# A hybrid mixer and feed-forward layer on one core: the down projection as seven products of half the size, on its whole depth, with its loads issued three products ahead

## The chip, the cores and the metric

The kernel runs on one core of one Trainium2 chip. The metric is the device time of one execution in microseconds (us), as the median of several executions on the chip. All arrays are fp32; a number that goes into a matmul is first split into a rounded part (hi, fp32r) and the rest (lo, fp32r), and one product of two tiles is three matmuls: hi by hi, hi by lo, lo by hi.

## The reference

One layer over 2048 tokens with 16 meta tokens ahead of them: a token mixer (a state-space branch and an mLSTM branch, merged and projected) and then a channel mixer. The change is in the channel mixer, and there in its last product:

```
def channel_mixer(x, g_pre, g_post, w_gate, w_up, w_conv, b_conv, w_down):
    h = rmsnorm(x, g_pre)
    a = causal_dwconv(h @ w_gate, w_conv, b_conv)
    y = (jax.nn.gelu(a, approximate=True) * (h @ w_up)) @ w_down
    return x + rmsnorm(y, g_post)
```

h has 1024 columns, w_gate and w_up are 1024 by 2816, w_down is 2816 by 1024. Below, y stands for the 2816-wide product that goes into w_down.

## The kernel before

The program is written in Python with a scheduler behind it: the order of the instructions on each engine is not the written one, but what the scheduler makes of it ahead of time. On the chip each engine then runs its own queue strictly in that order, with semaphores between the queues. All DMAs are issued by SP (the SyncE queue), in its order; an issue that has to wait holds up every issue behind it.

The mixer takes the first half of the program and is not touched. The feed-forward part has three stages.

- **Two passes of gate and up** (the loops over `m` in `range(NF)`, lines 1279 to 1303). Pass `p` takes half of the tokens; unit `m` makes 128 of the 2816 columns of y for them. Gate and up together are done by Strassen's algorithm: seven products named 1, 6, 2, 7, 5, 4, 3 instead of eight (`ffn_unit`, lines 1196 to 1262). In pass 0 each product is 24 matmuls that move 258 or 256 columns (two pieces of 12), in pass 1 it is 12 matmuls that move 512 columns. The activations are resident in 14 tiles `t0` to `t11`, `q0`, `q1`; the weights of each unit are loaded (`wg`, `wu`, lines 1131 and 1133), combined on VectorE and split on ScalarE and VectorE (lines 1124 and 1125). Each unit ends with a convolution, a Gelu and a product, in two halves, each stored to `y_d` in DRAM (line 1262).
- **The down projection** (lines 1311 to 1359). For each half `nh` of the output columns all 22 weight tiles of 128 by 512 are loaded through `mk`, split, and kept in `t0` to `t10`. Then for each of 16 token tiles three loads of y (8, 8 and 6 tiles of 128 by 128; `ys`, line 1335, two buffers) are split (`yhl`, ScalarE on line 1338, VectorE on line 1339), and 66 matmuls (lines 172 to 174) that move 512 columns add into one PSUM tile.
- **The end of each token tile** (lines 1344 to 1359): a square with sum, the gain, and for the second half the norm, `h1_d` loaded as a tile of 128 by 1024 and added, and two stores.

The tiles `mk` (three buffers of 128 by 2080), `dw` (tags `ws`, `wh`, `wl`, two buffers each) and `du`, `dx` (the units' own) share the on-chip memory with the 14 resident tiles. The helper `mm3` emits the three matmuls of a product, `mm3x` the same for Strassen's sums.

## Time and profile before

| | us |
|---|---|
| median of 3 runs | 2793.52 (2791.82 to 2795.34) |
| the profiled execution, its own time | 2792.36 |
| its span, first to last instruction | 2790.6 |
| TensorE busy in the span | 2759.1 |
| VectorE / ScalarE busy | 1761.1 / 1054.7 |
| gate and up, pass 0: first matmul | 1403.8 |
| gate and up, pass 1: last convolution starts | 2304.7 |
| down projection: first matmul to start of the last | 2287.3 to 2783.3 |

In a row of a window table stand the window, its length, then for PE (matmuls), PEld (weight loads of TensorE), DVE (VectorE), ACT (ScalarE) and POOL (GpSimd) the busy time and in brackets the number of instructions, then the granted clock of TensorE as a share of full speed, the busy share of the DMA engines and GB/s. Matmuls overlap each other in the array, so the duration of one is no measure of the rate; the count in a window without idle time is. In an answer on one line or tile, three durations in ns stand as smallest, middle and largest.

### The profile page before, as it was taken

The page shows a single profiled execution, that of the slowest core. Times are in us where ns is not written, and L with a number is a line of the kernel's source. Part 1 is how long each engine was busy: PE and PEld are TensorE (multiplying, and loading weights), DVE is VectorE, ACT ScalarE, POOL GpSimd, SP SyncE. Part 2 cuts the span into 40 slices and gives each one's busy share as a digit, 9 for nine tenths or more (in the row PEclk, how much of TensorE's full clock was granted, in tenths as well). Part 3 has the DMA queues.
Part 4 walks back from the last instruction along what each step waited for, and adds up shares of the span by engine and source line. Part 5 has one row for each costly group of instructions (what it writes and reads, how often), then busy time and mean ns, then how long its engine had stood idle before and what let it go on. Part 6 is the DMA issues. An engine that isn't in the chain of part 4 may idle for free.

```text
span 2790.6 us, 40815 instructions
## 1 busy us (share of the span) xinstructions
PE 2759.1 (99%) x15590; PEld 2484.9 (89%) x15590; DVE 1761.1 (63%) x3429; ACT 1054.7 (38%) x1979; POOL 136.8 (5%) x225
## 2 busy tenths in 40 slices
...
GB/s 309 106 79 131 158 147 121 71 69 72 145 159 144 167 212 121 223 196 250 265 157 138 159 234 87 73 176 85 80 80 81 79 145 149 99 90 165 157 166 128
DMA packets 323478, 395.47 MB, mean 142 GB/s; under 512 B 40321, under 2 KB 229142, under 8 KB 322642
## 3 DMA queue, kind: packets, MB, share of 16 engines
...
## 4 chain that ended last, share of the span: by engine, by line
PE 82%; DMA 7%; DVE 6%; ACT 1%; issue 1%; POOL 1%; SPq 0%; DVEq 0%; POOLq 0%; ACTq 0%
PE mm L172 10%; PE mm L174 10%; PE mm L173 10%; PE ac L173 9%; PE ac L174 9%; PE ac L172 8%; PE ac L179 4%; PE ac L178 4%; PE ac L177 4%; PE mm L177 3%; PE mm L179 3%; PE mm L178 3%; DMA wu<-in_w_up_dram 2%; DMA gat<-gab_d 1%; DVE w L1125 1%
## 5 line engine op out<-in xcount | busy, mean ns | idle before, releaser
L174 PE MATMUL mm<-hTh,wl 128*128 128x410 f32 (+3 forms) x1216 | 428.0, 352 | 0.0
L172 PE MATMUL mm<-hTh,wh 128*128 128x410 f32 (+3 forms) x1216 | 427.6, 352 | 0.0
L173 PE MATMUL mm<-hTl,wh 128*128 128x410 f32 (+3 forms) x1216 | 427.4, 352 | 0.0
L1339 DVE TENSOR_TENSOR yhl<-ys,yhl 128x1024 fp32r<-128x1024 f32 (+1 forms) x96 | 109.1, 1137 | 291.9 <-ACT yhl L1338 291.9
L173 PE MATMUL ac<-t,yhl 128*128 128x512 f32 x704 | 278.5, 396 | 0.0
L174 PE MATMUL ac<-t,yhl 128*128 128x512 f32 x704 | 277.3, 394 | 0.0
L172 PE MATMUL ac<-t,yhl 128*128 128x512 f32 x704 | 276.6, 393 | 0.0
L177 PE MATMUL mm<-t,w 128*128 128x258 f32 (+2 forms) x792 | 253.7, 321 | 3.5 <-DVE u L1226 2.6
L178 PE MATMUL mm<-t,w 128*128 128x258 f32 (+2 forms) x792 | 253.5, 320 | 0.4 <-DVE t L1069 0.4
L177 PE MATMUL ac<-t,w 128*128 128x258 f32 (+2 forms) x792 | 253.2, 320 | 0.6 <-ACT u L1217 0.6
L179 PE MATMUL ac<-t,w 128*128 128x258 f32 (+2 forms) x792 | 253.1, 320 | 0.1
L179 PE MATMUL mm<-t,w 128*128 128x258 f32 (+2 forms) x792 | 252.5, 320 | 0.7 <-DVE w L1125 0.7
L178 PE MATMUL ac<-t,w 128*128 128x258 f32 (+2 forms) x792 | 253.1, 320 | 0.0
L173 PEld LDWEIGHTS mm<-hTl,wh 128*128 128x128 f32 x1216 | 228.7, 188 | 2.6
L174 PEld LDWEIGHTS mm<-hTh,wl 128*128 128x128 f32 x1216 | 228.8, 188 | 2.3
L172 PEld LDWEIGHTS mm<-hTh,wh 128*128 128x128 f32 x1216 | 228.7, 188 | 2.0
L1338 ACT ACTIVATE yhl<-ys 128x1024 fp32r<-128x1024 f32 (+1 forms) x96 | 95.0, 990 | 348.4 <-PE ac L173 345.9
L156 ACT ACTIVATE wh<-ws 128x1024 fp32r<-128x1024 f32 x104 | 109.9, 1059 | 237.8 <-PE mm L173 137.5
L1124 ACT ACTIVATE w<-s 128x512 fp32r<-128x512 f32 x176 | 109.3, 628 | 164.7 <-DVE s L1139 70.3
L177 PEld LDWEIGHTS mm<-t,w 128*128 128x128 f32 x792 | 149.7, 189 | 18.0 <-DVE u L1226 4.4
L172 PEld LDWEIGHTS ac<-t,yhl 128*128 128x128 f32 x704 | 132.4, 188 | 32.3
L177 PEld LDWEIGHTS ac<-t,w 128*128 128x128 f32 x792 | 149.2, 189 | 13.0 <-ACT u L1217 1.1
...
## 6 DMA issues: line engine op xcount, KB each, us to landing
ys<-y_d SPq DMA_DIRECT2D x64, 512.0 KB, 3.7
wg<-in_w_gate_dram SPq DMA_DIRECT2D x44, 512.0 KB, 3.6
wu<-in_w_up_dram SPq DMA_DIRECT2D x44, 512.0 KB, 4.3
...
ws<-in_w_m_dram SPq DMA_DIRECT2D x32, 512.0 KB, 3.8
ws<-in_w_ba_dram SPq DMA_DIRECT2D x32, 512.0 KB, 4.0
ws<-in_w_out_dram SPq DMA_DIRECT2D x32, 512.0 KB, 5.3
gat<-gab_d SPq DMA_DIRECT2D x48, 256.0 KB, 4.8
```

The costliest lines, as they stand in the source:

```text
L156: S.activation(wh, ws, AF.Copy, scale=scale)
L172: T.matmul(out=ps, lhsT=lh, rhs=rh, start=first, stop=False)
L173: T.matmul(out=ps, lhsT=lh, rhs=rl, start=False, stop=False)
L174: T.matmul(out=ps, lhsT=ll, rhs=rh, start=False, stop=last)
L177: T.matmul(out=ps, lhsT=lh, rhs=rh, start=first, stop=False, skip_group_check=True)
L178: T.matmul(out=ps, lhsT=lh, rhs=rl, start=False, stop=False, skip_group_check=True)
L179: T.matmul(out=ps, lhsT=ll, rhs=rh, start=False, stop=last, skip_group_check=True)
L1124: S.activation(t[:, 0], src, AF.Copy)
L1125: V.tensor_tensor(t[:, 1], src, t[:, 0].bitcast(F32), ALU.subtract)
L1338: S.activation(yh, ys, AF.Copy)
L1339: V.tensor_tensor(yl, ys, yh.bitcast(F32), ALU.subtract)
```

## The change

The down projection is done by Strassen's algorithm. The 2816 rows of w_down are cut in two halves of 11 tiles, and its columns within each half `nh` in two halves of 256; two token tiles that lie four apart are taken together. Seven products (in the order 1, 6, 2, 7, 5, 4, 3) then stand for eight. One product is 11 tiles deep: 33 matmuls that move 256 columns. There are 2 halves of 8 units of 7, so 112 products.

What the products need is made ahead:

- `down_weight_sums`: in pass 0 of gate and up, units 1 to 4 and 14 to 21, the four sums of weight blocks are made on VectorE and stored to `wt_d`.
- `down_input_sums`: in pass 1, the four sums of y blocks are made and stored to `s_d`, one depth tile in each unit. The last one (`last_sums`) is made inside the down projection, since its y comes last.
- `turn_down`: while the last unit of pass 1 runs, 8 of the 11 weight tiles of six products are loaded through `mk` and split into `t0` to `t11`. The other 3 tiles of each product (`rest_piece`, tiles `x1` to `x7`) and product 3's 8 (`main_piece`, `q0`, `q1`) come in the down projection's first products. For the second half of the columns all 21 pieces are loaded again inside the stage, over the products that end the first half and begin the second, as the list `cut` deals them out.

The pools `mk` and `dw` are now closed ahead of the down projection, and a new pool `dn` takes their place. In it lie three buffers `raw` of 128 by 1408 through which everything passes that is split: the input of each product (128 by 1408 from `y_d` or `s_d`), the weight pieces (128 by 1024 and 128 by 768), and the two tiles of `last_sums`; and two tiles `st0`, `st1` of split input, which products take in turn. `st_load(i + 3)` is issued at product `i`, `st_split(i + 1)` too. The output of the first half of the columns goes to `yo_d` in DRAM and is read back (`y0`, one buffer) by `finish`, which reads `h1_d` in two halves through one buffer `ht`; the stores wait in the list `later` until products 1 and 3 of what follows.

The core of the diff (the removed stage is shown above):

```diff
+    s_d = dp.tile([8, 4, 128, 11, 128], F32, name="s_d")
+    wt_d = dp.tile([2, 4, 128, 11, 256], F32, name="wt_d")
+    yo_d = dp.tile([16, 128, 512], F32, name="yo_d")
...
+    def down_input_sums(p, m):
+        t = mk_tile()[:, 0:2048]
+        for h in range(2):
+            P.dma_start(out=t[:, h * 1024:h * 1024 + 1024], in_=y_d[m + 11 * h, :, p * 1024:(p + 1) * 1024])
+        yield
+        a11, a21, a12, a22 = (t[:, i * 512:i * 512 + 512] for i in range(4))
+        V.tensor_tensor(a22, a21, a22, ALU.add)
+        V.tensor_tensor(a21, a11, a21, ALU.subtract)
+        V.tensor_tensor(a11, a22, a11, ALU.subtract)
+        V.tensor_tensor(a12, a12, a11, ALU.subtract)
+        yield
+        for i, a in enumerate((a11, a21, a12, a22)):
+            P.dma_start(out=s_d[p * 4:p * 4 + 4, i, :, m, :].rearrange("j p t -> p j t"),
+                        in_=a.rearrange("p (j t) -> p j t", j=4))
...
+    ORDER = (1, 6, 2, 7, 5, 4, 3)
...
+    def split(hi, lo, raw):
+        S.activation(hi, raw, AF.Copy)
+        V.tensor_tensor(lo, raw, hi.bitcast(F32), ALU.subtract)
...
+    def turn_down():
+        for n in ORDER[:6]:
+            t = mk_tile()[:, 0:2048]
+            P.dma_start(out=t.rearrange("p (k n) -> p k n", k=8), in_=down_src(0, n, 0, 8))
+            places(n)
+            for h in range(2):
+                main_split(n, h, t[:, h * 1024:h * 1024 + 1024])
...
-        ffn_unit(1, m, op1, wt)
+        i = m - 1 if m < 12 else m - 12
+        piece_turn(down_input_sums(int(m >= 12), i) if m else None)
+        ffn_unit(1, m, op1, wt, turn_down if m == NF - 1 else None)
+        piece_sums()
+    piece_turn(None)
     phX.close()
-    el = pool(ctx, "el", bufs=2)
+    phM.close()
+    phW.close()
...
+    dn = pool(ctx, "dn")
+
+    PR = [(nh, j, n) for nh in range(2) for j in range(8) for n in ORDER]
...
+    def raw_tile():
+        return dn.tile([128, 1408], F32, tag="raw", name="raw", bufs=3)
...
+    def st_split(i):
...
+        st = dn.tile([128, 2, 1408], F32R, tag=f"st{turn_[0] % 2}", name="st")
+        split(st[:, 0], st[:, 1], raw_of.pop(i))
...
+    def rest_piece(nh, n):
+        raw = raw_tile()[:, 0:768]
+        P.dma_start(out=raw.rearrange("p (k n) -> p k n", k=3), in_=down_src(nh, n, 8, 11))
+        wrest[n] = dn.tile([128, 2, 768], F32R, tag=f"x{n}", name=f"x{n}")
+        split(wrest[n][:, 0], wrest[n][:, 1], raw)
...
+        def prod(ps, n, first):
+            i = PR.index((nh, j, n))
+            st_load(i + 3)
+            for f in before(i):
+                f()
+            st_split(i + 1)
+            st = st_of.pop(i)
+            for k in range(11):
+                mm3x(ps, st[:, 0, k], st[:, 1, k], moving(n, 0, k), moving(n, 1, k), first and k == 0, k == 10)
+            if n in (1, 3):
+                while later:
+                    later.pop(0)()
...
+    def finish(t, o1):
+        sm = dn.tile([128, 1], F32, tag="sm", name="sm", bufs=2)
+        V.tensor_reduce(out=sm, in_=sq4[t], op=ALU.add, axis=mybir.AxisListType.X)
+        rs = rstd_of(Small(dn, "r", 2), sm, 128, 1, 1.0 / D)
+        y0 = dn.tile([128, 512], F32, tag="y0", name="y0")
+        P.dma_start(out=y0, in_=yo_d[t])
+        for hh, src in ((1, o1), (0, y0)):
+            cs_ = slice(hh * 512, hh * 512 + 512)
+            ht = dn.tile([128, 512], F32, tag="ht", name="ht")
+            P.dma_start(out=ht, in_=h1_d[NM + t * 128:NM + (t + 1) * 128, cs_])
+            V.scalar_tensor_tensor(src, src, rs, ht, ALU.mult, ALU.add)
+            later.append(lambda cs_=cs_, src=src: P.dma_start(out=out[t * 128:(t + 1) * 128, cs_], in_=src))
...
+        if i < 6:
+            q = ORDER[i + 1]
+            f = [lambda: rest_piece(0, q)]
+            if i in (3, 4):
+                f.append(lambda: main_piece(0, 3, i - 3))
+        elif i in (9, ):
+            f = [last_sums]
+        elif first_i < i < last_i + 7:
+
+            f = second[cut[i - first_i - 1]:cut[i - first_i]]
...
+    cut = [0, 0, 2, 3, 5, 6, 8, 9, 12, 14, 16, 18, 21, 21]
```

Three places show how the order of the instructions changes. The first is VectorE's queue where pass 1 of gate and up ends. Before, from the last sum that waits for a product of gate and up (line 1236) on; `yhl` is the split of y for the down projection, and the first two of these stand ahead of this row:

```order
L1329 TENSOR_TENSOR t10_22848<-mk_22846,t10_22848 128x512 x2
L1261 TENSOR_TENSOR cc_22745<-cc_22745,u1_22650 128x512
L1236 TENSOR_TENSOR gp_22646<-ac_22705,u2_22651 128x512
L1256 SCALAR_TENSOR_TENSOR cc_22752<-gp_22646,cwf_89,cc_22752 128x512 x2
L1339 TENSOR_TENSOR yhl_22945<-ys_22942,yhl_22944 128x1024
L1261 TENSOR_TENSOR cc_22752<-cc_22752,u3_22652 128x512
```

Now, from the same sum (line 1276, after product 3 of the last unit) to the split of the first product's input; `t9` and `t11` are weights that `turn_down` splits, `mk_23001` the sums of y:

```order
L1276 TENSOR_TENSOR gp_23004<-ac_23063,u2_23009 128x512
L1155 TENSOR_TENSOR mk_23001<-mk_23001 128x512
L1381 TENSOR_TENSOR t9_23138<-mk_23135,t8_23137 128x1024
L1156 TENSOR_TENSOR mk_23001<-mk_23001 128x512
L1381 TENSOR_TENSOR t9_23138<-mk_23135,t8_23137 128x1024
L1296 SCALAR_TENSOR_TENSOR cc_23158<-gp_23004,cwf_92,cc_23158 128x512
L1381 TENSOR_TENSOR t11_23146<-mk_23143,t10_23145 128x1024
L1296 SCALAR_TENSOR_TENSOR cc_23158<-gp_23004,cwf_92,cc_23158 128x512
L1381 TENSOR_TENSOR t11_23146<-mk_23143,t10_23145 128x1024
L1301 TENSOR_TENSOR cc_23158<-cc_23158,u3_23010 128x512
L1381 TENSOR_TENSOR st_23182<-raw_23180,st_23182 128x1408
L1381 TENSOR_TENSOR st_23209<-raw_23185,st_23209 128x1408
```

Four splits and two sums now stand between the last sum of gate and up and its last product (line 1301), and no split of input stands ahead of it. On SP the same end, before, with the first loads of y for the down projection (`ys`) between the last stores of y:

```order
L1335 DMA ys_22854<-y_d_71 128x8x128
L1322 DMA mk_22822<-in_w_down_dram 128x4x512
L1335 DMA ys_22884<-y_d_71 128x8x128
L1262 DMA y_d_71<-cc_22599 128x512
L1322 DMA mk_22834<-in_w_down_dram 128x4x512
```

and now:

```order
L1302 DMA y_d_71<-cc_23151 128x512
L1159 DMA s_d_72<-mk_23001 128x4x128 x3
L1302 DMA y_d_71<-cc_23158 128x512
L1426 DMA raw_23180<-y_d_71 128x11x128
L1428 DMA raw_23185<-s_d_72 128x1408
L1426 DMA raw_23187<-y_d_71 128x11x128
L104 DMA g4_23194<-in_g_ffn_post_dram 128x512
L1546 DMA ht_25954<-h1_d_66 128x512
L1449 DMA raw_23189<-in_w_down_dram 128x3x256
L1428 DMA raw_23202<-s_d_72 128x1408
L1449 DMA raw_23204<-wt_d_73 128x768
```

The first load of input now stands behind the very last store of y, `cc_23158`; the weight rests (line 1449) alternate with inputs from then on. The second place is SP where the weights of the second half of the columns come in. Before, four loads of 128x4x512 and one of 128x2x512 (three of them shown) between loads of y:

```order
L1335 DMA ys_24329<-y_d_71 128x8x128
L1322 DMA mk_24297<-in_w_down_dram 128x4x512
L1335 DMA ys_24359<-y_d_71 128x8x128
L1322 DMA mk_24309<-in_w_down_dram 128x4x512
L1322 DMA mk_24321<-in_w_down_dram 128x2x512
```

Now, the first twelve of a stretch of 32 loads into `raw` (11 inputs on lines 1426 and 1428, 21 weight pieces on lines 1442 and 1449):

```order
L1426 DMA raw_25383<-y_d_71 128x11x128
L1442 DMA raw_25385<-in_w_down_dram 128x4x256
L1442 DMA raw_25391<-in_w_down_dram 128x4x256
L1428 DMA raw_25434<-s_d_72 128x1408
L1449 DMA raw_25436<-in_w_down_dram 128x3x256
L1426 DMA raw_25479<-y_d_71 128x11x128
L1442 DMA raw_25481<-wt_d_73 128x1024
L1442 DMA raw_25487<-wt_d_73 128x1024
L1428 DMA raw_25531<-s_d_72 128x1408
L1535 DMA yo_d_74<-o_25297 128x512
L1449 DMA raw_25533<-wt_d_73 128x768
L1426 DMA raw_25578<-y_d_71 128x11x128
```

Each of these loads takes one of the same three buffers. The third place is the end of SP's queue, about the last inputs. Before:

```order
L1335 DMA ys_25874<-y_d_71 128x8x128
L1355 DMA ht_25938<-h1_d_66 128x1024
L1335 DMA ys_25904<-y_d_71 128x6x128
L1359 DMA out_0_dram<-ht_25837 128x512 x2
L1359 DMA out_0_dram<-ht_25938 128x512 x2
```

and now:

```order
L1428 DMA raw_28069<-s_d_72 128x1408
L1548 DMA out_0_dram<-y0_27936 128x512
L1546 DMA ht_28197<-h1_d_66 128x512
L1542 DMA y0_28195<-yo_d_74 128x512
L1546 DMA ht_28200<-h1_d_66 128x512
L1548 DMA out_0_dram<-o_27944 128x512
L1548 DMA out_0_dram<-y0_28195 128x512
L1546 DMA ht_28250<-h1_d_66 128x512
L1542 DMA y0_28248<-yo_d_74 128x512
L1546 DMA ht_28253<-h1_d_66 128x512
L1548 DMA out_0_dram<-o_27945 128x512
L1548 DMA out_0_dram<-y0_28248 128x512
```

Loads of `ht` and `y0`, each into the one buffer of its name, now stand between the stores.

210 lines of the change are left out of this document (156 added, 54 removed).

## The prediction

> **What bounds the kernel now.** I read the profile's page first, then windows of single stages, then the rows of the instructions that the change makes larger or moves.
>
> ```profile
> span 2790.6 us, 40815 instructions
> PE 2759.1 (99%) x15590; PEld 2484.9 (89%) x15590; DVE 1761.1 (63%) x3429; ACT 1054.7 (38%) x1979; POOL 136.8 (5%) x225
> PE 82%; DMA 7%; DVE 6%; ACT 1%; issue 1%; POOL 1%; SPq 0%; DVEq 0%; POOLq 0%; ACTq 0%
> ```
>
> TensorE is busy for 99% of the span and holds 82% of the chain that ends last. The windows tell at which rate it works: one in pass 0 of gate and up, one in pass 1, one in the down projection, and the last.
>
> ```profile
> core 0: us, PE busy (x) PEld busy (x) DVE busy (x) ACT busy (x) POOL busy (x), PEclk, DMA share, GB/s
> 1750.00:1800.00 50.00, 50.00 (x420) 50.00 (x419) 37.45 (x73) 20.42 (x36) 0.56 (x3) 1.00 0.27 85
> 2100.00:2150.00 50.00, 50.00 (x217) 40.36 (x216) 33.62 (x54) 18.76 (x31) 2.19 (x2) 1.00 0.26 82
> 2400.00:2450.00 50.00, 50.00 (x217) 40.44 (x216) 13.87 (x14) 12.28 (x18) 0.00 (x0) 1.00 0.32 95
> ```
>
> Without idle time a matmul that moves 512 columns takes 50/217 = 0.2304 us, one that moves 256 or 258 takes 50/420 = 0.1190. The down projection waits for nothing today: VectorE is busy for 13.9 of 50 us there, ScalarE for 12.3.
>
> **The gain.** The old stage is three groups of 704 matmuls, of which this is one:
>
> ```profile
> L173 PE MATMUL ac<-t,yhl 128*128 128x512 f32 x704 | 278.5, 396 | 0.0
> ```
>
> That is 2112 x 0.2304 = 486.6 us. The new one is 112 products of 33, 3696 x 0.1190 = 439.8 us. **Gain: 46.8 us**, if TensorE still waits for nothing. One product lasts 33 x 0.1190 = 3.93 us.
>
> **What a tile costs on its way in.** Each tile in `raw` is loaded, rounded on ScalarE and subtracted on VectorE; only then can its buffer be loaded anew. The durations for 768 (smallest) and 1024 columns (middle), and the landing times:
>
> ```profile
> L1338 ACT ACTIVATE yhl<-ys x96: 831/1060/1064, 2277.5 to 2773.8; 128x1024 fp32r<-128x1024 f32 x64, 128x768 fp32r<-128x768 f32 x32
> L1339 DVE TENSOR_TENSOR yhl<-ys,yhl x96: 949/1226/1227, 2285.9 to 2774.7; 128x1024 fp32r<-128x1024 f32 x64, 128x768 fp32r<-128x768 f32 x32
> ys<-y_d SPq DMA_DIRECT2D x64, 512.0 KB, 3.7
> ys<-y_d SPq DMA_DIRECT2D x32, 384.0 KB, 3.2
> out_dram<-ht SPq DMA_DIRECT2D x32, 256.0 KB, 2.2
> wi<-win_d SPq DMA_DIRECT2D x8, 256.0 KB, 2.5
> ```
>
> ScalarE adds 229 ns and VectorE 277 ns for 256 columns, so 1408 columns are estimated at 1.40 and 1.64 us; 128 KB more add 0.5 us, so the 704 KB of an input land in an estimated 4.4. The turnover of a buffer is then 4.4 + 1.40 + 1.64 = 7.4 us for an input, 3.7 + 1.06 + 1.23 = 6.0 for 128x1024 of weights, 3.2 + 0.83 + 0.95 = 5.0 for 128x768.
>
> In the steady state three buffers hold: 7.4 us is less than three products (11.8). A split begins when the product two back has ended, and needs 1.40 + 1.64 = 3.0 us, at most 0.4 more for a copy ahead of it, against 3.93: it hides too. So units 2 to 6 of the first half should run at TensorE's rate. The stalls are elsewhere, in seven terms.
>
> **1. The gap between the stages.** The rows of a sum, a convolution step and two plain operations of 512 columns on VectorE:
>
> ```profile
> L1256 DVE SCALAR_TENSOR_TENSOR cc<-gp,cwf,cc 128x512 f32<-128x512 f32 x88 | 66.0, 749 | 8.7 <-ACT cc L1254 8.5
> L1261 DVE TENSOR_TENSOR cc<-cc,u 128x512 f32<-128x512 f32 x44 | 30.3, 688 | 0.1
> L1138 DVE TENSOR_TENSOR s<-wu 128x512 f32<-128x512 f32 x44 | 30.5, 693 | 52.2 <-DMA wu<-in_w_up_dram 52.2
> ```
>
> By the order, after the last matmul of gate and up VectorE does four operations of 0.69 (sum, two of `mk`, the last product), two of 0.75 and four weight splits of 1.23: 2.8 + 1.5 + 4.9 = 9.2 us. The last of these frees the store of `cc_23158`, and only behind that store does SP issue the first input: 4.4 + 1.40 + 1.64 = 7.4 more, all with TensorE idle. 16.6 us and issues, say 17; bounds 15 (part of the weight splits ready ahead) and 22 (the weight loads late, as they wait in the same queue). Today the inputs are loaded ahead of the last stores and this costs nothing. The idle clock adds to it:
>
> ```profile
> 1370.00:1375.00 5.00, 2.05 (x10) 1.39 (x9) 5.00 (x8) 1.06 (x1) 2.33 (x1) 1.00 0.99 348
> 1375.00:1380.00 5.00, 5.00 (x16) 3.93 (x17) 4.21 (x7) 0.65 (x2) 2.85 (x3) 0.66 0.48 148
> ```
>
> After 3 us of idle time the granted clock is 0.66 over the next 5 us, with 16 matmuls where 22 fit: 1.4 to 1.7 us lost. I take **18 us** for the gap.
>
> The Trainium skill (TensorE: Matmul & The Clock Gate, Part 1: The HAM clock gate) has the same rule: about 3.4 us of idle time halve the clock until some 3.4 us of work have passed. It would charge about 1.7 us for each such gap, and the two rows agree.
>
> **2. The first weights.** In the first seven products 7 inputs, 7 rests and 2 pieces of product 3 pass through three buffers: (7 x 7.4 + 7 x 5.0 + 2 x 6.0)/3 = 33 us against 7 x 3.93 = 27.5. That is 5.5 if no buffer ever waits. One does: an input that has landed holds its buffer until the product two back frees its `st`. With two buffers left, input and rest one after another take 12.4/2 = 6.2 us a product, 16 us over seven. I take **12**.
>
> **3. The last sums** (product 3 of the second unit). A y tile loads (3.7), four sums (4 x 0.69 = 2.8), a store (2.2), the input loads again from `s_d` (4.4), and splits (3.0): 16 us in a row. It begins when the input of product 7 has been split, so 7 and 4 lie beside it: 7.9. **9 us** with what VectorE's sums delay; bounds 4 and 14.
>
> **4. The second weights.** 14 pieces of 1024, 7 of 768 and 11 inputs pass through the three buffers: (14 x 6.0 + 7 x 5.0 + 11 x 7.4)/3 = 67 us, dealt out over products 51 to 61, which last 11 x 3.93 = 43. So 24 us if nothing waits; weights also wait for the last product that reads their place, and one queue holds up the next. **28 us**; bounds 15 (an early start) and 40.
>
> **5. The second half's norm.** `finish` adds to SP's queue two `y0`, four `ht` and four stores a unit, which wait for VectorE and for each other; an input behind them has about 3 us of slack. By the order the split of line 1547 that waits for `ht` also stands ahead of sums that TensorE waits for. No row shows this; from 0 to 3.5 us a unit over seven units (one 256 KB landing of 2.5 and one operation of 0.75), nearer the middle: **12 us**, bounds 0 and 25. No gain is possible, since nothing is taken out there.
>
> **6. The tail.** Today, from the last matmul:
>
> ```profile
> 2783.34 0.39 PE L174 MATMUL ac<-t,yhl 128*128 128x512 f32 x1
> 2785.57 0.55 POOL L107 TENSOR_TENSOR rs<-ms,neghalf 128x1 f32<-128x1 f32 x1 [13.50 <-DVE ms L105]
> 2786.16 1.41 DVE L1358 SCALAR_TENSOR_TENSOR ht<-o,rs,ht 128x512 f32<-128x512 f32 x2 [0.73 <-POOL rs L107]
> 2786.94 0.99 SPq L1359 DMA_DIRECT2D out_dram<-ht  x2
> ```
>
> 6.9 us to the span's end. Now two tiles end at once, with one `ht` and one `y0`: three loads in a row (2.5 and 0.4 of issue each) and two operations of 0.75 more: **10 us**; bounds 8 and 13.
>
> **7. Gate and up.** Four more sums of 0.69 in 12 units of pass 0 (20 us each) and in 21 of pass 1 (19.4 us each): VectorE's 37.5 of 50 us in pass 0 become 37.5 + 4 x 0.69 x 50/20 = 44.4, its 33.6 in pass 1 40.7. Under 90%, so mostly hidden; but its queue runs later. **4 us**, bounds 0 and 12.
>
> Sum: -46.8 + 18 + 12 + 9 + 28 + 12 + 10 + 4 = **+46 us**. The profiled execution took 2792.36 (1.8 around its span), 1.2 below the median of 2793.52; so 2838.6 for a profile, and 2839.7 as a median: **2840 us**. All low ends together (15, 5.5, 4, 15, 0, 8, 0 = 47.5) give no change; all high ends (22, 16, 14, 40, 25, 13, 12 = 142) give 2889.
>
> **The rivals.**
>
> *The loads keep ahead.* If landings are short, the buffers turn over in time: in the second weights, 32 tiles in 43 us leave 4.0 us a tile and buffer, where 6.3 are needed, so a load would have to land 2.3 us sooner than the rows say. For it: DMA is busy for a third of the time today, so there is room. Against it: the waits are of one load after another, not of volume. With terms 2 to 5 and 7 gone, 2793.5 - 46.8 + 28 = 2775 us. Chance 0.14.
>
> *The clock falls in every stall.* Slower still: if the 3 us gaps of terms 2, 3 and 4, about a dozen, each cost the 1.7 us of the rows above on the path, 20 us come on top: 2860. Against it: where loads set the pace, slower matmuls hide in part. Chance 0.10. The Trainium skill's rule quoted above (TensorE: Matmul & The Clock Gate, Part 1: The HAM clock gate) speaks for this one.
>
> *The change does not do what it says.* The loads are issued three products ahead only if a buffer is free; if SP's queue itself is the bound in the second half, inputs come late in every product there, 2 us each over 49 products: 2840 + 98 - 12 = 2926. The slack of 3 us speaks against it. Chance 0.04. Terms that happen to cancel within 0.2% (5.6 us, about what a measurement of this kernel can tell from no change): 0.04.
>
> **How the numbers follow.** The forecast has 0.68 and holds 2800 to 2885. Faster is the first rival, 0.14; the same 0.04; slower the rest, 0.68 + 0.10 + 0.04 = 0.82. The range leaves out the first and the third rival: 2795 to 2885.
>
> **What would show it.** Right: in the profile after, TensorE at 3696 matmuls of 0.119 us; a gap of some 17 us ahead of the first of them; idle time before matmuls on the tiles `x` and `t` in the first and the eighth unit, released by VectorE's split, and none in units 2 to 6; a clock below 1 behind the gap; 17 us from the last matmul to the end. Wrong: a stage of under 460 us from its first matmul to its last, or stalls spread evenly over all units.

## The result, and the profile after

The changed kernel takes 2913.8 us (median of 4 runs, 2909.45 to 2916.42), the kernel before 2792.7 beside it: a ratio of 1.0431, 95% interval 1.0413 to 1.0449. It is slower by 121 us. The forecast was 2840 (2795 to 2885), slower with a chance of 0.82: the side is right, the size is not. Its profiled execution has a span of 2913.9 us, 123.3 more than before's 2790.6.

The page of the changed kernel, the lines that answer to those of before (span; busy time of the engines; the chain that ended last):

```profile
span 2913.9 us, 45019 instructions
PE 2763.7 (95%) x17174; PEld 2563.7 (88%) x17174; DVE 1966.3 (67%) x3691; ACT 1138.1 (39%) x2073; POOL 134.2 (5%) x225
PE 58%; DMA 20%; DVE 15%; ACT 3%; issue 3%; SPq 1%; POOL 0%; DVEq 0%; ACTq 0%; POOLq 0%
```

TensorE's share of the chain fell from 82% to 58%; transfers (20%) and VectorE (15%) took it. The windows tell where. Gate and up, two windows each in pass 0 and pass 1; then the down projection in a quiet stretch, at its start, where the second weights come in, and in the second half:

```profile
1450.00:1500.00 50.00, 45.43 (x364) 44.79 (x363) 41.56 (x81) 20.08 (x38) 3.70 (x5) 0.97 0.83 271
1750.00:1800.00 50.00, 50.00 (x420) 50.00 (x419) 37.27 (x72) 22.13 (x41) 0.56 (x3) 1.00 0.25 80
1900.00:1950.00 50.00, 46.29 (x188) 35.78 (x187) 41.45 (x69) 16.38 (x27) 3.68 (x2) 0.97 0.97 301
2100.00:2150.00 50.00, 50.00 (x217) 40.51 (x216) 34.05 (x55) 18.35 (x31) 2.19 (x2) 1.00 0.30 99
2450.00:2500.00 50.00, 50.00 (x426) 50.00 (x425) 27.82 (x30) 21.01 (x30) 0.00 (x0) 1.00 0.66 201
2350.00:2375.00 25.00, 20.36 (x123) 19.25 (x123) 10.11 (x9) 8.88 (x11) 0.00 (x0) 0.76 0.65 206
2625.00:2675.00 50.00, 34.15 (x169) 30.63 (x167) 24.06 (x27) 18.50 (x23) 0.55 (x1) 0.62 0.61 197
2700.00:2800.00 100.00, 91.99 (x722) 90.25 (x721) 54.17 (x73) 36.58 (x51) 3.23 (x6) 0.95 0.73 232
```

Read the matmul counts. 420, 217 and 426 are the full rates, so the quiet windows (1750, 2100, 2450) run as forecast, the last a little faster (the forecast had 420). The others do not: in 1900:1950 there are 188 matmuls, where before had, in the same window,

```profile
1900.00:1950.00 50.00, 50.00 (x216) 40.50 (x215) 33.59 (x55) 18.87 (x31) 2.19 (x2) 1.00 0.25 77
```

In that window the changed kernel has a DMA share of 0.97 where before had 0.25, and VectorE at 41.5 of 50 us where it had 33.6: the sums of eleven units run within five, from 1884 to 1970 us. The gap between the stages, on TensorE and on SP:

```profile
2334.05 0.40 PE L182 MATMUL ac<-q,w 128*128 128x512 f32 x1
2351.03 0.58 PE L180 MATMUL ac<-t,st 128*128 128x256 f32 x1 [16.59 <-ACT st L1380]
```

```profile
2343.58 0.33 SPq L1302 DMA_DIRECT2D y_d<-cc  x1
2344.01 0.38 SPq L1426 DMA_DIRECT2D raw<-y_d  x1
```

16.6 us idle, and the first load of input 0.4 us behind the last store of y, as forecast. VectorE's queue ahead of that store, from its last sum for gate and up to their last product, takes 9.1 us (forecast 9.2):

```profile
2334.48 0.69 DVE L1276 TENSOR_TENSOR gp<-ac,u 128x512 f32<-128x512 f32 x1 [0.30 <-PE ac L182]
2342.86 0.69 DVE L1301 TENSOR_TENSOR cc<-cc,u 128x512 f32<-128x512 f32 x1
```

The durations that the forecast estimated (input splits on VectorE and ScalarE, input loads):

```profile
L1381 DVE TENSOR_TENSOR st<-raw,st 128x1408 fp32r<-128x1408 f32 x112 | 181.7, 1624 | 110.0 <-ACT st L1380 109.7
L1380 ACT ACTIVATE st<-raw 128x1408 fp32r<-128x1408 f32 x112 | 154.1, 1378 | 200.1 <-PE mm L182 76.6
raw<-s_d SPq DMA_DIRECT2D x64, 704.0 KB, 4.6
raw<-y_d SPq DMA_DIRECT2D x48, 704.0 KB, 4.5
```

1.62, 1.38 and 4.5 us against estimates of 1.64, 1.40 and 4.4: the inputs were priced right. The other loads were not. From 2330 us on, as medians of the few landings that the trace has, weight pieces of 512 KB took 4.7 and 6.3 us (the forecast took 3.7 from other loads), those of 384 KB 3.4 and 3.8 (3.2), and `ht` 4.4 (2.5):

```profile
raw<-wt_d SPq DMA_DIRECT2D x8, 512.0 KB, 4.7
raw<-in_w_down_dram SPq DMA_DIRECT2D x8, 512.0 KB, 6.3
raw<-wt_d SPq DMA_DIRECT2D x8, 384.0 KB, 3.4
raw<-in_w_down_dram SPq DMA_DIRECT2D x6, 384.0 KB, 3.8
ht<-h_d SPq DMA_DIRECT2D x32, 256.0 KB, 4.4
```

More was wrong in how the parts meet. A stall in a unit of the second half shows it, VectorE and then TensorE:

```profile
2775.30 0.75 DVE L1547 SCALAR_TENSOR_TENSOR o<-o,rs,ht 128x512 f32<-128x512 f32 x1 [0.60 <-POOL rs L110]
2776.66 1.63 DVE L1381 TENSOR_TENSOR st<-raw,st 128x1408 fp32r<-128x1408 f32 x1 [0.60 <-ACT st L1380]
2779.27 0.75 DVE L1547 SCALAR_TENSOR_TENSOR y<-y,rs,ht 128x512 f32<-128x512 f32 x1 [0.99 <-DMA ht<-h_d]
2780.02 0.42 DVE L1514 TENSOR_TENSOR o<-mm,o 128x256 f32<-128x256 f32 x1
```

```profile
2780.50 0.38 PE L180 MATMUL mm<-t,st 128*128 128x256 f32 x1 [2.03 <-DVE o L1514]
```

VectorE waits for `ht`; the sum of line 1514 stands behind it; TensorE waits 2.0 us for that sum. In the tail the same operations wait one after another for one buffer:

```profile
2897.42 0.75 DVE L1547 SCALAR_TENSOR_TENSOR o<-o,rs,ht 128x512 f32<-128x512 f32 x1 [0.60 <-POOL rs L110]
2901.52 0.75 DVE L1547 SCALAR_TENSOR_TENSOR y<-y,rs,ht 128x512 f32<-128x512 f32 x1 [3.35 <-DMA ht<-h_d]
2905.88 0.75 DVE L1547 SCALAR_TENSOR_TENSOR o<-o,rs,ht 128x512 f32<-128x512 f32 x1 [3.61 <-DMA ht<-h_d]
2909.89 0.75 DVE L1547 SCALAR_TENSOR_TENSOR y<-y,rs,ht 128x512 f32<-128x512 f32 x1 [3.26 <-DMA ht<-h_d]
```

**The account, term by term.** From the starts of the matmuls in the timeline I take, for each stretch, its length less the number of its matmuls times 0.1190 us; call that its *loss* (idle time and slow clock together). A unit has 231 matmuls. Before, the down projection alone would begin at 2297.0 (its last matmul's start, 2783.34, less 2111 x 0.2304); after, gate and up let go of TensorE at 2334.3 (2334.05 and one matmul).

| term | forecast, with bounds | measured | how |
|---|---|---|---|
| gain of the matmuls | -46.8 | -46.8 | at the forecast's two rates (see below); units 3 to 7 run without loss (-1.2 in all) |
| 7, gate and up | 4 (0 to 12) | 37 | 2334.3 - 2297.0 |
| 1, gap, with its slow clock | 18 (15 to 22) | 20 | 16.7 idle, 3.3 slow |
| 2, first weights | 12 (5.5 to 16) | 16.5 | loss of unit 1, 19.8, less the 3.3 |
| 3, last sums | 9 (4 to 14) | 11 | loss of unit 2 |
| 4, second weights | 28 (15 to 40) | 46 | loss of products 50 to 64 |
| 5, second half's norm | 12 (0 to 25) | 28 | loss of products 65 to 112 |
| 6, tail | 10 (8 to 13) | 12 | 19.5 from the last matmul's start to the end, 7.3 before |

These add up, with the -1.2, to 123: the difference of the spans. Three terms make the miss: gate and up (33 too little), second weights (18) and the norm (16).

The two rates in this table are the forecast's, counts of a window of 50 us, and such a count takes in the matmuls that reach over its edges. By the starts of the matmuls the spacing is 0.2323 us before (from 2303.10 to 2783.34) and 0.1180 after (units 3 to 7). By these the gain is 54 us and not 47, the down projection alone would have begun at 2292.9 before, so term 7 is 41, and each unit loses 0.2 more; the total is the same.

### The profile page after: what moved, and what is told of

Same layout as the page of the kernel before. It is cut to its first block, busy times and chain, and to the rows that moved or that the text cites. A ratio compares the mean times of both kernels' runs of the same rounds, so it can differ in the third digit from the quotient of the medians.

```text
span 2913.9 us, 45019 instructions
## 1 busy us (share of the span) xinstructions
PE 2763.7 (95%) x17174; PEld 2563.7 (88%) x17174; DVE 1966.3 (67%) x3691; ACT 1138.1 (39%) x2073; POOL 134.2 (5%) x225
## 4 chain that ended last, share of the span: by engine, by line
PE 58%; DMA 20%; DVE 15%; ACT 3%; issue 3%; SPq 1%; POOL 0%; DVEq 0%; ACTq 0%; POOLq 0%
PE mm L175 9%; PE mm L177 9%; PE mm L176 9%; PE ac L182 4%; PE ac L180 4%; PE ac L181 4%; PE mm L180 3%; PE mm L181 3%; PE mm L182 3%; DMA wu<-in_w_up_dram 3%; PE ac L176 2%; PE ac L177 2%; PE ac L175 2%; DVE w L1165 2%; DMA mk<-y_d 2%
## 5 line engine op out<-in xcount | busy, mean ns | idle before, releaser
L180 PE MATMUL mm<-t,w 128*128 128x258 f32 (+2 forms) x792 | 257.9, 326 | 18.0 <-DVE u L1266 11.2
L180 PE MATMUL ac<-t,w 128*128 128x256 f32 (+2 forms) x792 | 254.5, 322 | 9.4 <-ACT w L1164 5.0
L181 PE MATMUL mm<-t,w 128*128 128x258 f32 (+2 forms) x792 | 256.7, 324 | 0.7 <-DVE t L1074 0.7
L182 PE MATMUL mm<-t,w 128*128 128x258 f32 (+2 forms) x792 | 255.4, 324 | 1.4 <-DVE w L1165 1.4
L182 PE MATMUL ac<-t,w 128*128 128x256 f32 (+2 forms) x792 | 253.5, 321 | 2.8 <-DVE w L1165 2.7
L1381 DVE TENSOR_TENSOR st<-raw,st 128x1408 fp32r<-128x1408 f32 x112 | 181.7, 1624 | 110.0 <-ACT st L1380 109.7
L181 PE MATMUL ac<-t,w 128*128 128x256 f32 (+2 forms) x792 | 253.5, 321 | 0.0
L1380 ACT ACTIVATE st<-raw 128x1408 fp32r<-128x1408 f32 x112 | 154.1, 1378 | 200.1 <-PE mm L182 76.6
L180 PEld LDWEIGHTS mm<-t,w 128*128 128x128 f32 x792 | 151.6, 191 | 35.5 <-DVE u L1266 6.9
L180 PEld LDWEIGHTS ac<-t,w 128*128 128x128 f32 x792 | 149.6, 189 | 23.3 <-ACT w L1164 6.3
L182 PEld LDWEIGHTS mm<-t,w 128*128 128x128 f32 x792 | 151.6, 192 | 14.3 <-DVE w L1165 2.1
L182 PEld LDWEIGHTS ac<-t,w 128*128 128x128 f32 x792 | 149.6, 189 | 16.0 <-DVE w L1165 4.4
L181 PEld LDWEIGHTS mm<-t,w 128*128 128x128 f32 x792 | 151.8, 192 | 12.7 <-DVE t L1074 0.9
L181 PEld LDWEIGHTS ac<-t,w 128*128 128x128 f32 x792 | 150.0, 189 | 11.5
```

What stands on the lines that cost most here:

```text
L180: T.matmul(out=ps, lhsT=lh, rhs=rh, start=first, stop=False, skip_group_check=True)
L181: T.matmul(out=ps, lhsT=lh, rhs=rl, start=False, stop=False, skip_group_check=True)
L182: T.matmul(out=ps, lhsT=ll, rhs=rh, start=False, stop=last, skip_group_check=True)
L1380: S.activation(hi, raw, AF.Copy)
L1381: V.tensor_tensor(lo, raw, hi.bitcast(F32), ALU.subtract)
```

## The experiments

The table has the measured quantity of each stage for the changed kernel and all runs: how late the last unit of pass 1 starts against before, the time from the last matmul of gate and up to the first of the down projection, and the losses. Times with one run are of a single execution. Eight runs share the code of gate and up with the changed kernel (E3, E4, E6, E7, E8, E11, E12 and it); their delay is 28.6 to 36.5, which is the scatter to read that column with. Their gap scatters from 14.4 to 18.2.

| | us | gate/up late | gap | unit 1 | unit 2 | 50 to 64 | 65 to 112 |
|---|---|---|---|---|---|---|---|
| changed kernel | 2913.8 | 33.0 | 17.0 | 19.8 | 10.9 | 46.3 | 28.0 |
| E1 loads one a unit | 2930.1 | 36.8 | 31.8 | 22.6 | 12.3 | 47.0 | 25.4 |
| E2 no arithmetic | 2898.0 | 17.9 | 15.6 | 19.9 | 7.5 | 46.5 | 30.0 |
| E3 no second weights | 2855.2 | 29.6 | 18.2 | 19.8 | 10.7 | -0.5 | 24.9 |
| E4 no norm loads | 2880.4 | 34.7 | 17.2 | 19.7 | 10.8 | 44.3 | 6.1 |
| E5 sums on POOL's queue | 2925.9 | 46.5 | 20.6 | 19.9 | 13.7 | 42.4 | 26.4 |
| E6 four buffers, no norm | 2838.3 | 28.8 | 17.4 | 12.1 | 2.9 | 28.5 | -0.2 |
| E7 weights on POOL's queue | 2909.5 | 28.6 | 17.6 | 23.5 | 15.3 | 45.2 | 23.5 |
| E8 small matmuls | 2904.5 | 36.5 | 17.1 | 18.9 | 11.9 | 43.5 | 22.6 |
| E9 arithmetic alone | 2922.7 | 40.4 | 17.9 | 22.4 | 10.0 | 47.8 | 31.5 |
| E10 no sums | 2868.7 | -4.1 | 15.2 | 20.5 | 8.4 | 48.0 | 27.0 |
| E11 four and three small | 2823.6 | 33.5 | 15.2 | 2.9 | 1.5 | 15.1 | 2.3 |
| E12 seven small | 2828.9 | 32.2 | 14.4 | 7.5 | 3.1 | 12.9 | 10.9 |
| E13 E11, sums on GpSimd | 2853.2 | 57.7 | 20.4 | 3.2 | 1.5 | 10.8 | 8.3 |
| E14 E13, one a unit | 2856.8 | 57.3 | 30.7 | 3.9 | 2.4 | 13.9 | 2.6 |
| E15 E13, first input on POOL | 2860.9 | 58.3 | 23.8 | 5.1 | -0.3 | 12.3 | 8.7 |
| E16 E11, sums held on VectorE | 2822.1 | 31.1 | 18.0 | 2.3 | 1.5 | 12.8 | 10.7 |
| E17 E16, five products ahead | 2832.1 | 37.4 | 16.7 | 6.4 | 6.6 | 14.1 | 6.0 |
| E18 E16, stores behind weights | 2797.6 | 6.8 | 16.2 | 4.0 | -0.3 | 16.5 | 3.7 |

### E1 to E4: a part spread, or taken out

E1, the loads of each piece behind the last store of y of the unit before:

```diff
         if new:
-            next(new)
+            with tc.issue_after(last_store[0].ins):
+                next(new)
```

> The loads of each weight sum and of each input sum are queued on SP behind the last store of y of the unit before, so that one piece falls in each unit, as the written order has it; nothing else changes. In the changed kernel gate and up end 37 us later than before; eleven input sums run there within five units, at a DMA share of 1.0. Theory (a burst of DMAs delays the weights of gate and up): with the pieces spread the DMA share stays near 0.5, and gate and up end at most 12 us later than before; the total falls by 20 to 30 us, to 2885 to 2895. Rival (four more operations a unit on VectorE, whenever they come): the delay stays within 5 us of 37, the total at 2910 to 2916.

Measured: 2930.1 us (ratio 1.0493, 1.0474 to 1.0511), gate and up 36.8 late, the gap 32 us since the last sums now come late too. Neither theory's time came. The DMA share in 1900:1950 is down to 0.49, so the burst was gone; the delay was not. A burst at a DMA share of 1 is what the window shows, and not, by itself, the cause.

E2, the sums without their operations:

```diff
-        V.tensor_tensor(a22, a21, a22, ALU.add)
-        V.tensor_tensor(a21, a11, a21, ALU.subtract)
-        V.tensor_tensor(a11, a22, a11, ALU.subtract)
-        V.tensor_tensor(a12, a12, a11, ALU.subtract)
```

> The eight operations of VectorE in the weight sums and the input sums are left out; loads and stores stay, so wt_d and s_d hold plain blocks and the result is not the layer's. Theory (burst of DMAs): gate and up still end 30 us or more later than before, the total stays above 2900. Rival (VectorE's operations): the delay falls under 10 us, the total to about 2880.

Measured: 2898.0, 17.9 late; between the two. Half of the delay needs VectorE's operations; half comes with transfers alone.

E3, the second half of the columns with the weights of the first:

```diff
-            f = second[cut[i - first_i - 1]:cut[i - first_i]]
+            f = []
```

> The 21 weight pieces of the second half of the columns are left out (their loads and splits); the second half multiplies with the weights of the first, so its columns are not the layer's. Theory (32 tiles pass through three buffers in 11 products): the stretch of products 50 to 64, which has 43 us of idle time and slow clock in the changed kernel, falls to 5 or less, and the total by 38 to 45, to 2870 to 2876; the stalls of the later units stay. Rival (the input loads are late there for the DMA queue's own sake, with stores of the first half and loads of the norm in it): more than 15 us stay in that stretch.

Measured: the loss of products 50 to 64 goes from 46.3 to -0.5. The whole of it is the second weights'. The total fell further than expected, to 2855.2: 47 of the 59 us come from here, the rest from gate and up, the norm and the tail, by 3 to 5 each in this one execution.

E4, `finish` without its loads:

```diff
-        P.dma_start(out=y0, in_=yo_d[t])
...
-            P.dma_start(out=ht, in_=h1_d[NM + t * 128:NM + (t + 1) * 128, cs_])
-            V.scalar_tensor_tensor(src, src, rs, ht, ALU.mult, ALU.add)
+            V.scalar_tensor_tensor(src, o1, rs, g4, ALU.mult, ALU.add)
```

> The loads of y0 and ht in the second half are left out: the norm's two operations read the output tile and the gains instead, with the same number of operations and stores, so the output is not the layer's. Theory (VectorE's queue waits for ht with sums behind it that TensorE waits for): the 32 us of idle time and slow clock in units 9 to 16 fall to under 8 and the tail from 19 to about 8; the total falls by 30 to 38, to 2876 to 2884. Rival (the inputs of the second half are late, since stores and loads share one queue): over 15 us stay in these units.

Measured: 2880.4, as the theory had it; products 65 to 112 lose 6.1 instead of 28.0, all of it in units 10 and 11, and from the last matmul's start to the end it is 7.5 us instead of 19.5. The window, to be held against the changed kernel's 722 matmuls above:

```profile
2700.00:2800.00 100.00, 96.45 (x812) 95.74 (x811) 64.72 (x88) 40.47 (x57) 4.36 (x8) 1.00 0.67 214
```

### E5 to E8: queue, buffers, clock

E5, the sums' loads and stores issued by GpSimd, four lines like this one:

```diff
-            P.dma_start(out=wt_d[nh, b, :, k:k + kn, :], in_=t[:, :, b])
+            G.dma_start(out=wt_d[nh, b, :, k:k + kn, :], in_=t[:, :, b])
```

> All loads and stores of the weight sums and input sums are issued by GpSimd (busy for 5% of the span) and not by SP; sizes, order and arithmetic stay. With one piece a unit but on SP, gate and up still ended 37 us later than before, so the burst is not the cause. Theory (SP's queue: stores that wait for the sums on VectorE stand ahead of the loads of gate and up's weights): gate and up end at most 12 us later than before, the total falls by 20 to 30 us, to 2885 to 2895. Rival 1 (VectorE has too little room for four more operations a unit): the delay stays within 8 us of 37. Rival 2 (DMA volume): the same, with the DMA share at 1.0 where the stalls are.

Measured: 2925.9, 46.5 late, above all three forecasts. Taking them off SP in this way does not help. (GpSimd also makes the copies of `halo` for each unit's convolution, which now stand behind its DMA issues, so the run bears on SP's queue from one side only; E18 returns to it.)

E6, four buffers; the room comes from `ht`, `y0` and half of the gains:

```diff
-        return dn.tile([128, 1408], F32, tag="raw", name="raw", bufs=3)
+        return dn.tile([128, 1408], F32, tag="raw", name="raw", bufs=4)
```

> As the run without the norm's loads (2880), with four buffers for raw instead of three. To make room the second half has no tiles ht and y0 either, one operation on VectorE instead of two and gains of 256 columns, so the output is not the layer's. Theory (turnover of three buffers sets the pace of the first and the second weights): the first unit's 20 us of idle time and slow clock fall to under 10, products 50 to 64 from 44 to 15 to 25; the total falls to 2845 to 2860. Rival (the one queue in which weights and inputs wait behind each other, or the DMA engines): both within 5 us of their value, the total at 2872 to 2882.

Measured: against E4, unit 1 loses 12.1 instead of 19.7, unit 2 loses 2.9 instead of 10.8, products 50 to 64 lose 28.5 instead of 44.3; total 2838.3. One buffer more is worth 31 us in these three. That they are a matter of turnover is shown; the first and the last are a little above what the theory expected, the total is under it, as gate and up and the later units lost less too.

E7, the weight pieces on another queue, same buffers:

```diff
-        P.dma_start(out=raw.rearrange("p (k n) -> p k n", k=4), in_=down_src(nh, n, 4 * h, 4 * h + 4))
+        G.dma_start(out=raw.rearrange("p (k n) -> p k n", k=4), in_=down_src(nh, n, 4 * h, 4 * h + 4))
```

> The weight pieces of the down projection (rests and main pieces, into the same three raw buffers) are issued by GpSimd, the inputs by SP as now. Theory (buffer turnover): products 50 to 64 keep 40 us or more of idle time and slow clock, total 2905 to 2920. Rival (one queue: an input waits behind a weight piece that waits for the last product that reads its place): under 25 us there, total 2885 to 2895.

Measured: 45.2 in products 50 to 64, total 2909.5, as the theory had it. One queue was not the limit there.

E8, TensorE kept busy in the stalls of products 55 to 64:

```diff
+            if 55 <= i < 65:
+                tw = pst("tp", [128, 128])
+                with tc.issue_after(end_mm[0].ins):
+                    for _ in range(12):
+                        T.transpose(tw, ident, ident)
```

> Twelve small matmuls (the identity by itself, into a PSUM tile that nobody reads) are put in TensorE's queue ahead of each of products 55 to 64, behind the last matmul of the product before; they take some 2 us a product in time in which TensorE is idle now. Nothing else changes. Theory (the slow clock after each stall is on the path): of the 46 us in products 50 to 64 about 20 are matmuls at a lower clock; these fall to under 8, and the total by 6 to 14 us, to 2900 to 2908. Rival (the loads set the pace there, and slower matmuls hide in the wait for them): the total stays within 4 us of 2914, with more idle time in place of the slow clock, or rises by the small matmuls.

Measured: 2904.5 (2895.95 to 2905.84; ratio 1.0385, 1.0364 to 1.0406). The row of the small matmuls alone in 2600:2700: 16.8 us, and a clock of 0.88, where the changed kernel has 0.78 and 0.77 in the halves of this window:

```profile
2600.00:2700.00 100.00, 16.79 (x120) 15.33 (x120) 0.00 (x0) 4.03 (x18) 0.88 0.73 236
```

Yet products 50 to 64 lose 43.5 instead of 46.3: of the 9.3 us by which the total fell, 2.8 are there, the rest in later units and in the tail, which this does not touch. TensorE's idle time in that stretch falls from 25 to 16 us, but the small matmuls take 17; what is lost to a slow clock falls from some 21 to some 10. So the loads set the pace there, and a faster clock mostly buys longer waits. The total is inside the theory's window, the place is not; neither forecast is met whole, and the place speaks for the rival.

### E9 and E10: what gate and up wait for

E9, the operations alone; nothing is loaded or stored for them, and products read blocks in place of sums. The operations of the last ten units are held behind the last one of the unit before; those of the first eleven are not:

```diff
-        for h in range(2):
-            P.dma_start(out=t[:, h * 1024:h * 1024 + 1024], in_=y_d[m + 11 * h, :, p * 1024:(p + 1) * 1024])
...
+        c = ident.unsqueeze(1).to_broadcast([128, 4, 128])
+        for i in range(4):
+            V.tensor_tensor(t[:, i * 512:i * 512 + 512].rearrange("p (q n) -> p q n", q=4), c, c, ALU.subtract)
```

> The weight sums and the input sums keep their operations on VectorE (four of 512 columns each, on the identity, into a tile of mk) and lose all loads and stores; products that took sums read blocks of w_down or of y instead, so the output is not the layer's, and the last sums feed nobody. Spreading the pieces (37 us of delay left) and GpSimd's queue (46) did not help gate and up, and without the arithmetic 18 of 33 us were left. Theory (the transfers: they slow the loads of gate and up's weights and hold their queue, and the sums on VectorE only stretch that): gate and up end at most 8 us later than before. Rival (VectorE's room): 12 us or more. In both, the second unit's 11 us fall to under 2, since no product waits for the last sums.

Measured: 2922.7, 40.4 late. The rival is right about VectorE. The window of E9:

```profile
1900.00:1950.00 50.00, 41.75 (x155) 32.36 (x154) 48.39 (x81) 14.46 (x24) 10.09 (x2) 0.87 0.16 52
```

DMA share 0.16, and 155 matmuls where 217 fit: VectorE is full (48.4 of 50), since the ready sums stand together at the head of its queue: 44 operations between 1894 and 1933 us. In the changed kernel the same 44 wait for loads and take from 1884 to 1970, so E9 shows that VectorE's order can cost this much, not that it alone did. On one point both sides were wrong: unit 2 still loses 10.0, though no product waits for the last sums any more.

E10, no sums in gate and up at all:

```diff
-        piece_turn(down_input_sums(int(m >= 12), i) if m else None)
```

> Neither weight sums nor input sums in gate and up: no loads, no operations, no stores; the down projection reads blocks instead, so the output is not the layer's. What is left of the delay of gate and up is that of the weights loaded in the last unit. Theory (the sums make the delay): gate and up end 3 to 8 us later than before. Rival (the last unit's weight loads and splits make a large part of it): 12 us or more.

Measured: 2868.7, and gate and up 4.1 us early, in the same window at full rate:

```profile
1900.00:1950.00 50.00, 50.00 (x217) 40.48 (x216) 32.31 (x53) 19.07 (x31) 2.19 (x2) 1.00 0.29 89
```

The whole of term 7 is the sums'; the weights loaded in the last unit cost nothing there, as the last matmul of gate and up starts at 2289.5, ahead of the 2297.0 of before.

### E11 and E12: smaller buffers

E11; inputs in two pieces, weights in pieces of three tiles, and the norm's loads through `rw`:

```diff
-    def raw_tile():
-        return dn.tile([128, 1408], F32, tag="raw", name="raw", bufs=3)
+    def raw_tile(tag="rw"):
+        return dn.tile([128, 768], F32, tag=tag, name=tag, bufs=4 if tag == "ri" else 3)
...
+        for a, b in ((0, 6), (6, 11)):
+            raw_of[i].append(raw_tile("ri")[:, 0:(b - a) * 128])
...
-        y0 = dn.tile([128, 512], F32, tag="y0", name="y0")
+        y0 = raw_tile()[:, 0:512]
-            ht = dn.tile([128, 512], F32, tag="ht", name="ht")
+            ht = raw_tile()[:, 0:512]
```

> A correct kernel: the three raw buffers of 1408 columns become seven of 768, four for inputs (each input in two pieces of 768 and 640 columns), three for weight pieces (now 768, 768, 512 and 768 columns), for the last sums and for the norm's loads, whose own two buffers go. Theory (turnover of buffers; smaller pieces come round sooner): first unit's 20 us fall to under 12, products 50 to 64 from 46 to 15 to 30, the norm's 28 us in units 10 to 16 to under 12 since its loads no longer wait for each other; total 2840 to 2870. Rival (what counts is how long one transfer takes, and twice as many take longer): within 8 us of 2914, with stalls in units 3 to 7 too, where two inputs' buffers leave little room.

Measured: 2823.6, better than expected: unit 1 loses 2.9, unit 2 loses 1.5, products 50 to 64 lose 15.1, the rest 2.3. E11's windows where the second weights end and in the second half:

```profile
2650.00:2700.00 50.00, 50.00 (x426) 50.00 (x425) 32.84 (x55) 22.94 (x42) 1.65 (x3) 1.00 0.87 288
2700.00:2800.00 100.00, 99.80 (x842) 99.19 (x840) 67.10 (x116) 44.39 (x82) 4.39 (x8) 1.00 0.88 281
```

Nearly the same memory (three of 1408 columns, `ht` and `y0` against seven of 768) in more and smaller buffers, with the same bytes, brings the loss of the whole down projection from 104 us to 22. Units 4 to 7 show no stall, unit 3 has 0.8.

E12, all seven in one rotation, inputs two products ahead:

```diff
-            st_load(i + 3)
+            st_load(i + 2)
```

> A correct kernel: seven buffers of 768 columns for all of it in turn, inputs written two products ahead instead of three; pieces as in the run with four and three. Theory: as there, products 50 to 64 at 15 to 30, no stall in units 3 to 7; total 2835 to 2865. Rival: a weight piece waits for the buffer of an input that is not split yet, as it is with three buffers, and 35 us or more stay in products 50 to 64.

Measured: 2828.9; less loss in products 50 to 64 (12.9), more after (10.9), where norm and inputs share the rotation. Buffers of their own for the inputs are no worse.

### E13 to E18: gate and up again, on top of E11

E13, the eight operations on GpSimd:

```diff
-        V.tensor_tensor(a22, a21, a22, ALU.add)
+        G.tensor_tensor(a22, a21, a22, ALU.add)
```

> A correct kernel: that with four and three small buffers (2823.6), and in it the arithmetic of the weight sums and input sums of gate and up on GpSimd instead of VectorE; loads and stores stay on SP, in the same bunches. Theory (VectorE's queue: sums that are ready early or wait for a load stand ahead of operations for which TensorE waits): gate and up end 8 to 20 us later than before and not 33, the 18 of the run without arithmetic being the nearest; total 2800 to 2815. Rival (the transfers, whoever adds): within 6 us of 33, total 2818 to 2830.

Measured: 2853.2, 57.7 late; both sides missed. The reason shows in VectorE's own rows. The same split of 512 columns between 1880 and 1990 us, first in E13, then in the changed kernel:

```profile
L1165 DVE TENSOR_TENSOR w<-s,w 128x512 fp32r<-128x512 f32 x18 | 22.2, 1241 | 0.0
```

```profile
L1165 DVE TENSOR_TENSOR w<-s,w 128x512 fp32r<-128x512 f32 x19 | 12.9, 689 | 0.0
```

An operation of VectorE that reads two tiles on chip takes 1.24 us here instead of 0.69. The mean is of two kinds: by the timeline, six of the eighteen splits take 0.68 us, and twelve, which overlap a sum of GpSimd for 0.6 us or more, take 1.16 to 1.78. So VectorE is no freer than before (48.6 of 50 us busy in 1900:1950). The Trainium skill (SBUF — State Buffer, Summary: rules for kernel authors) says that a GpSimd operation and a VectorE operation with two inputs there shut each other out until one has ended; the two rows agree. The run does not tell the theories apart.

E14, E13 with E1's edit:

```diff
+            with tc.issue_after(last_store[0].ins):
+                next(new)
```

> A correct kernel: as the run with the sums on GpSimd, and the loads of each piece queued on SP behind the last store of y of the unit before. Theory (what is left with the arithmetic off VectorE are bunched transfers, at a DMA share of 1.0): gate and up end at most 8 us later than before; the gap may grow by the last sums, as it did from 17 to 32 us with the pieces spread and the arithmetic on VectorE; total 2795 to 2815. Rival (stores that wait for their sums hold up the weights behind them on SP, bunched or not): the delay stays at that of the bunched run or above.

Measured: 2856.8, 57.3 late, the gap 31. The delay is that of E13, as the rival had it. VectorE is not full here: 37.1 of 50 us in 1900:1950, where TensorE has 213 matmuls, and the splits of 512 columns above take 0.68 us between 1880 and 1990. What SP waits for speaks for the rival too, as shown under E18.

E15, E13 with the first input, and in the same way the first rest, issued by GpSimd:

```diff
-                P.dma_start(out=dst, in_=y_d[m0 + a:m0 + b, :, c0:c0 + 128].rearrange("m p t -> p m t"))
+                (G if i == 0 else P).dma_start(out=dst, in_=y_d[m0 + a:m0 + b, :, c0:c0 + 128].rearrange("m p t -> p m t"))
```

> A correct kernel: as the run with the sums on GpSimd, and the first input and the first weight rest of the down projection issued by GpSimd, so that they do not stand behind the last store of y on SP. Theory (the order of SP's queue makes the gap): the gap of 15 us between the last matmul of gate and up and the first of the down projection falls to 7 to 11, as VectorE's splits and last products still stand ahead; the total falls by 4 to 8 against the run with the sums on GpSimd. Rival (VectorE's queue makes it): within 2 us of 15.

Measured: 2860.9, the gap 24 and not 7 to 11. The load was moved behind something later: GpSimd issues it at 2373.09, when its four last sums are done, and VectorE's last product ends at 2372.0. So the run does not clear SP; that SP's order alone makes the gap is not shown.

E16, the sums held back on VectorE, and the weight sums moved to units 10 to 21:

```diff
+        pin = last_mul[0]
         ffn_unit(1, m, op1, wt, turn_down if m == NF - 1 else None)
-        piece_sums()
+        with tc.issue_after(pin.ins) if m < 12 else ExitStack():
+            piece_sums()
...
-        w_piece = wsum.pop(0) if 1 <= m < 5 or 14 <= m < 22 else None
+        w_piece = wsum.pop(0) if 10 <= m < 22 else None
```

> A correct kernel: that with four and three small buffers (2823.6), and in it the sums stay on VectorE but each piece's operations are queued behind the last operation of the unit before (the weight sums and the first eleven input sums, whose data is there long ahead), and the weight sums move to units 10 to 21 of pass 0, one each. Loads and stores follow by their buffers. Theory (bunching: the scheduler puts ready sums ahead of what TensorE waits for): gate and up end 5 to 15 us later than before, in place of 33; total 2796 to 2808. Rival (VectorE's time as such, or stores on SP ahead of weights): 28 us or more, as with one piece a unit on SP; total above 2818.

Measured: 2822.1, 31.1 late, but with the delay in another place: at the end of pass 0 it is 1.0 where the changed kernel has 11.8, and pass 1 adds 30 in steps of 1 to 5 us. There TensorE waits for splits of gate and up's weights (engine, line, what it waited for: us, times, longest, 1870 to 2325 us):

```profile
PE ac L180 <- ACT w L1164: 9.3, 8, 1.8
PE ac L180 <- ACT u L1259: 5.0, 5, 1.6
```

Delay and total are the rival's. The theory holds for pass 0 (by the holding back or by the other units; the run has both), and in pass 1 something else takes over: the weights come late.

E17, E16 with five products in `turn_down`:

```diff
-        for n in ORDER[:6]:
+        for n in ORDER[:5]:
...
-            if i in (3, 4, 5):
-                f.append(lambda: main_piece(0, 3, i - 3))
+            f.append(lambda: main_piece(0, ORDER[5 + i // 3], i % 3))
```

> A correct kernel: as the run with the sums held on VectorE, and only five products' weights loaded during the last unit of pass 1 instead of six; product 4's come in three pieces over the first products, as product 3's do. Theory (two splits of 1.2 us on VectorE and one load fewer stand in the gap): the gap falls by 2 to 4 us, the last unit's delay by 1 to 3, the first unit's stalls grow by 0 to 4; total 2790 to 2804. Rival (the gap is set by the last store of y and the load behind it): the gap stays within 1 us, the total within 3 us of the run beside it.

Measured: 2832.1 (2819.95 to 2832.91; ratio 1.0122, 1.0094 to 1.0149), the gap 16.7 against 18.0, units 1 and 2 lose 9 us more. Neither forecast came, and the gap's change is within its scatter. The last two weight splits are late instead (VectorE waits 2.0 us for ScalarE's half of the first), so the last product starts at 2342.92, 11 us behind the last matmul; what the splits are worth in the gap stays open.

E18, E16 with the stores of sums, and the loads of the next piece, behind a later unit's weights on SP:

```diff
-        if piece_at[0]:
-            next(piece_at[0], None)
-        piece_at[0] = new
-        if new:
-            next(new)
+        with tc.issue_after(last_wu[0].ins):
+            if piece_at[1]:
+                next(piece_at[1], None)
+            piece_at[:] = [new, piece_at[0]]
+            if new:
+                next(new)
```

> A correct kernel: as the run with the sums held on VectorE (2822.1; gate and up 31 us late, 30 of them in pass 1), and on SP the stores of each piece's sums, and the loads of the next piece, are queued behind the loads of a later unit's weights (wu), the stores one unit later than now, so that no weight load stands behind a store that waits for VectorE. Theory (SP's queue: weights behind stores of sums): gate and up end 3 to 12 us later than before, total 2793 to 2805. Rival (transfers take the weights' bandwidth, or VectorE's time as such): 25 us or more, total above 2815.

Measured: 2797.6 (2791.77 to 2800.04), a ratio of 1.0008 (0.9999 to 1.0017) to before; gate and up 6.8 late. E18's window, with all the sums still in it:

```profile
1900.00:1950.00 50.00, 50.00 (x216) 40.47 (x215) 41.94 (x68) 19.56 (x34) 0.98 (x2) 1.00 0.53 169
```

VectorE is as busy as in the changed kernel (41.9 and 41.5), the same bytes move, and TensorE waits for nothing. So neither VectorE's time nor the transfers were too much: the order in two queues was. SP's own waits show its part. Where nothing else is in the way, SP stands waiting until a buffer for the weights of gate and up (`wg`, `wu`) comes free, and issues their loads at once. These waits of SP, first in E16, then in E18, 1870 to 2290 us:

```profile
SPq L1171 <- DVE s L1232: 26.8, 20, 2.5
SPq L1173 <- DVE w L1165: 16.6, 11, 6.5
SPq L1175 <- DVE w L1165: 105.5, 20, 10.1
SPq L1173 <- DVE s L1234: 65.2, 20, 6.2
```

That is 43 us in E16 and 171 in E18. Before it is 182, in E10 181, in E9, which has VectorE's bunch but no transfers, 172; in the changed kernel it is 87, in E2 86, in E14 58. Where it is short, SP waits for sums and for transfers of sums in its place, and the weights behind them go out late. Sums stood ahead of what TensorE needs, on VectorE (E9, E16's pass 0), and stores that wait for sums stood ahead of weight loads, on SP (E18 against E16). Mending VectorE's order alone leaves 31 us (E16); SP's alone was not tried in a clean form, since E5 burdened GpSimd. The 18 us that transfers alone cost (E2) fit with SP's part, and so does E1, where the burst was gone and the stores still stood ahead.

## Why the prediction was wrong

**The gain** is right in kind: units 3 to 7 run at TensorE's rate, without a stall. That unit 2 stalls was term 3. Its size was 54 us and not 46.8, since the two rates were read from counts of windows.

**Term 7, gate and up** (4, measured 37) is the step that failed. It reads: under 90%, so mostly hidden. It spread four operations a unit evenly over units by the written order. The scheduler did not: sums whose data is ready go to the head of the queue, eleven pieces in five units, and there they stand ahead of what TensorE waits for, although VectorE is busy for 41.5 of 50 us, no more than in E18. And the term looked at VectorE alone; it did not ask what stands behind the sums' stores on SP, though the weights of gate and up do, each with one unit's time to land. E10 gives the size, E9, E16 and E18 the cause. By the starts of the units, some 12 us of it arise in pass 0, 14 in the first five units of pass 1 and 7 in the last eight; how they divide between the two queues is not shown.

**Term 4, second weights** (28, bounds 15 to 40; measured 46). Mechanism right: E3 takes the term away, E6 and E11 shrink it by buffers alone, E7 shows that it was not the queue. The size failed in the sum 67 - 43 = 24 with 4 for waiting. Two things were too small. The weight pieces land later than it took: with the medians above the sum is 76 - 43 = 33, an estimate from few landings. And a buffer that waits for a place, or for the product two back, is idle: some 13 us are left for that, not 4. Term 2 (12, measured 16.5) is short too; how much of that is which is not shown.

**Term 5, the norm** (12, bounds 0 to 25; measured 28). The mechanism, VectorE held by `ht` ahead of sums that TensorE waits for, is right (rows above, E4). Three things were short. `ht` takes 4.4 us to land and not 2.5. Units 10 to 15 each have one wait of TensorE for such a sum, of 1.1 to 2.5 us, 11 in all; 10 more go into waits for splits of the inputs, which the term let hide in their slack of 3 us. And a wait of 2 us can be followed by 1.5 us lost to a slow clock, which the term priced at nothing: of the 28 us, 21 are idle time and 7 are not.

**Term 3** (9, measured 11) had the right size and the wrong reason. It added up the 16 us from the load of y to the split of product 10. With nobody waiting for those sums (E9, E10) unit 2 still loses 8 to 10; with one buffer more it loses 3 (E6). It is the two buffers that `last_sums` takes, not the chain through it.

**Terms 1 and 6** (18 and 10, measured 20 and 12) are right. The rows of the gap follow the path that the forecast gave: VectorE's queue to 2343.55, the store at 2343.58, the load at 2344.01, the first matmul at 2351.03. Which change of order would shorten it is not shown, since E15 and E17 moved other work into its place. The tail scatters: in E3, E7 and E8, which share its code, it is 15 us and not 19.5, so term 6 was met only within that.

**The rivals.** The loads keep ahead: no; it needed the landings to be shorter, and they were as estimated for the inputs and longer for the weights. The clock falls in every stall: the nearer of them in kind. Of the 104 us lost in the down projection, the rows of TensorE show 61 as idle time; the other 43 are matmuls at a lower clock. But where loads set the pace they mostly hide (E8), and the two largest misses, the order in the queues and the buffers, are not the clock's. SP's queue as the bound in the second half (2926, near in number): no; products between the stalls run at full rate and E7 changed nothing. The faster case never came, but E18 stands within 0.2% of before with the change's gain in it: the 46.8 are there, and what is still lost is 16 in the gap, 16 in products 50 to 64, 10 in gate and up and some 10 in the rest.
